# A planner's table of durations and its priorities set anew in a two-layer diffusion transformer kernel

## The chip, the core and the metric

The kernel runs on one core of a Trainium2 chip. The metric is the device time of one execution in microseconds (us), as the median of several runs. A core has five engines that each execute their own instructions strictly in order: TensorE (PE, matrix products into PSUM banks; its weight loads are listed as PEld), VectorE (DVE), ScalarE (ACT), GpSimd (POOL) and SyncE (SP), whose queue issues the transfers here. Engines wait for one another through semaphores, so an instruction that isn't ready holds up everything behind it on its engine.

## What is computed

Two layers over 512 latent and 256 context tokens of width 1024, with the same weights for both streams. The reference, cut to one layer's frame:

```python
m_lat = jnp.split(s_lat @ w_ada[li] + b_ada[li], 6, axis=-1)      # adaLN: six sections, also m_ctx
h = rms_norm(x, g_mix[li]) * (1.0 + m_lat[1]) + m_lat[0]
p = h @ w_in[li]                                                  # four groups of columns
y = jnp.concatenate([fourier_mix(..), diff_attention_latent(..), na_attention_latent(..), chunk_gmlp(..)], axis=-1)
x = x + m_lat[2] * (y @ w_out[li])
h = rms_norm(x, g_ffn[li]) * (1.0 + m_lat[4]) + m_lat[3]
x = x + m_lat[5] * conv_ffn(h, ffn_up[li], ffn_conv[li], ffn_conv_b[li], ffn_down[li])   # inner width 2816
```

The second layer needs the context only for its keys and values. Everything is float32; to keep that precision, a large product is three products of float32r operands, each operand being split into a high part and a low part.

## The kernel before

The streams lie feature-major in SBUF, eight tiles of 128 features. Products accumulate in eight PSUM banks. A product over 128 features is three matmuls (`mm3`: high by high, high by low, low by high).

**Weights.** `w_stream` fetches the weights in quarters of 128 x 512 into the four buffers `raw`. `w_split` makes the two parts of each in one of six pairs `wq`: ACT copies the high part, and a subtraction gives the low part, on DVE or POOL.

**adaLN.** `ada_wide` computes half a section of the modulation vectors on DVE, by product-sums over 128 x 512 tiles of the transposed weights. A tile serves one product-sum, or two where both streams need it. The tiles come through three buffers `wa`, one after another at a pace (`ada_loader`, first number of `pace` for layer 0 from a start time, last number for layer 1, begun with layer 0's FFN). In the trace such a product-sum is CUSTOM_DVE_ANT_0, with a short DVE_READ_ACCUMULATOR2_ANT behind it; in the listing of the order both are called ISA.

**Main stream.** One thread, `main`, walks through units in the order of the strings `o0` and `o1` (one for each layer): DQ, DK, DV are query, key and value projections of differential attention, NQ, NK, NV those of neighbourhood attention, GU and GV the two halves of the gating MLP, FA and FC the two halves of Fourier mixing, OO the out-projection. The letter behind says for which streams. The FFN follows, in 22 steps: `up` (two blocks of 128 channels), `conv` and `gated` on ACT, DVE and POOL, and now and then a `down` for four steps; `lead` says how many steps `up` runs ahead. The second layer's FFN begins in two halves of tokens, so its norm (`Norm`) has two parts: a sum of squares, a matmul with `ones`, a power on POOL (`mhalf`), a matmul that spreads the result over the partitions (`ident`), and then eight chunks that DVE and ACT scale, shift and split.

**Order.** Next to the main stream run threads for the results of each unit (`qk_post`, `copy_post`), attention items, gates, norms and weight splits. A thread offers one instruction at a time. The class `Sched` takes the thread whose instruction could start first by the planner's clock, or, among those that could start within `slack` of that, the one of the smallest number in `pr`. An instruction's duration in this plan is `Eng.cost`. Where the same work can go to two engines (`Alt`), the planned end plus a bias decides (`bias_w` for the weight subtractions: so many us are added to DVE's end). The instructions of each engine are then issued in the order of the plan; at run time only semaphores decide when they run. `items` and `heads` bound the attention items under way, `res_b` and `keep` hold back SBUF for them. All instructions are recorded in line 311 of the kernel before (line 314 of the changed one), so the trace is read by tiles, not by lines.

Of the kernel before, what the change touches and what calls it, by code (L numbers as in the profile page):

```python
# [11 lines left out]
F32R = mybir.dt.float32r  # L12
# [15 lines left out]
P = {"sb": 14016, "sr": 25920, "res_b": 1920, "res_r": 0, "res_p": 0, "heads": 2, "items": 8, "slack": 0.12,  # L28
     "pace": (5.5, 45.0, 6.5), "bias": {'DVE': 0.3}, "bias_w": {'DVE': 4.6}, "nk": 1,
     "st": (0, 0.2, 0, 0.3, 0.6, 0.4, 0.5),  # L30
     "pr": {'d': 1.5, 'n': 0.5, 'g': 2.11, 'gate': 3.5, 'w': 6.5, 'y': 0.01, 'conv': 0.51, 'gated': 0.01, 'main': 4.9, 'f': 3.5, 'fm': 7.7, 'ad': 0.01, 'an': 1.11, 'ada': 9.7},
     "o0": 'DKj4 DVj2 DQi GUj NKl FAj NKc GVj FCc NVl NQj NVc XX FCl OOc OOl',
     "o1": 'DKj2 GUl2 DQl DVj NKi NVi FAl NQl GVl XX FCl OOa OOb', "lead": 4, "ffn_s": (1, 0), "tail": [],
     "parts": [1, 1, 2], "uph": 2, "ada0": [[[1, 0, 1], [0, 0, 0]], [[1, 1, 1], [0, 1, 0]]], "seg": 0, "early": 1,
     "keep": 2080, "across": 1, "step": 4}
# [6 lines left out]
class Op:  # L42
    """One or more instructions of one engine, not yet issued."""
# [15 lines left out]
class Alt:  # L59
    """The same work on either of several engines."""  # L60
# [5 lines left out]
class Req:  # L66
    """A buffer of n elements per partition of an arena, wanted once some tiles have been written."""
# [6 lines left out]
class Arena:  # L74
    """Buffers of any length cut from one tile, short ones from its end."""
# [12 lines left out]
    def place(self, n, now):  # L88
        """The place for n grains that is free first, and when."""
# [83 lines left out]
class Eng:  # L173
    """An engine; its instructions come back as Ops."""
# [25 lines left out]
    def cost(self, op, aps, nkw, kw):  # L200
        n = max(elems(x) for x in aps)
        ps = any(x.tensor.name == self.psum for x in aps)
        if self.name == "PE":
            n = elems(aps[0])
            if op == "transpose":
                return 0.056 if aps[1].dtype == F32R else 0.11
            return max(0.109, n / 2400.0 + 0.0025) if aps[1].dtype == F32R else max(0.214, n / 597.0)
        if self.name == "DVE":
            if op == "tensor_copy":
                return 0.068 + n / (960.0 if ps else 1920.0)  # L210
# [1602 lines left out]
```

## Time and profile before

| what | value |
|---|---|
| median of 3 runs | 1694.07 us (1693.99 to 1695.23) |
| span of the profiled execution | 1691.7 us, 26998 instructions |
| PE busy | 1614.1 us, 95% |
| DVE busy | 1081.3 us, 64% |
| ACT busy | 753.5 us, 45% |
| POOL busy | 746.9 us, 44% |
| granted PE clock, mean | 0.981 of full speed |

The median is 2.4 us above the profiled span; that is what lies around the first and the last instruction. The mean shares hide the stages: the mixers of layer 0 end near 336 us, its out-projection at 446, its FFN at 1022; the mixers and the out-projection of layer 1 end near 1321, and its FFN fills the rest. A granted clock of 1.00 is 2.4 GHz and of 0.50 is 1.2 GHz; a stretch in between has had both.

### The profile page before, as it was taken

The numbers are of one execution on the slowest core, as the hardware profiler recorded it, in microseconds if no ns is written. First come the engines' busy times: TensorE is split into PE (matmuls) and PEld (weight loads), VectorE is DVE, ScalarE is ACT, GpSimd is POOL, SyncE is SP. The second block draws the span as 40 slices with busy tenths as digits, with TensorE's granted clock in tenths as the row PEclk, the third lists the DMA queues.
The fourth block names the chain that finished last, engine by engine and source line by source line (L and its number), as shares of the span: only waits on it lengthen the run. The fifth ranks groups of instructions, "written<-read, shape, count | busy, mean of one in ns | idle before, by whom it ended". The sixth has DMA issues, their size and how long they took to land.

```text
span 1691.7 us, 26998 instructions
## 1 busy us (share of the span) xinstructions
PE 1614.1 (95%) x9932; PEld 1431.5 (85%) x9932; DVE 1081.3 (64%) x2132; ACT 753.5 (45%) x1481; POOL 746.9 (44%) x585
## 2 busy tenths in 40 slices
PE   6889999999999999999999998899998999999999
PEld 2779988898788888888888888899998888888887
DVE  6989997797886555445454569697576544434334
ACT  3437663674433313233232335476675543433431
POOL 4782345526433333323233346632438744444442
PEclk9899999999999999999999998999999899999999
DMA  7432223445433333333333342410324433333232
GB/s 251 146 100 69 59 87 95 129 141 197 127 125 100 101 100 105 101 104 103 97 103 100 101 136 82 124 44 26 116 100 142 140 108 96 96 98 100 94 99 87
DMA packets 101652, 183.03 MB, mean 108 GB/s; under 512 B 12176, under 2 KB 14864, under 8 KB 101520
## 3 DMA queue, kind: packets, MB, share of 16 engines
q1 hardware_dynamic: 101520, 181.31, 34.1%
q8 instruction: 78, 1.28, 0.3%
q14 instruction: 54, 0.44, 0.1%
HBM read 177.07 MB, written 4.19 MB: 107 GB/s over the span
## 4 chain that ended last, share of the span: by engine, by line
PE 77%; DVE 14%; POOL 3%; DMA 2%; issue 2%; ACT 2%; SPq 0%; POOLq 0%; ACTq 0%; DVEq 0%
PE banks L311 77%; DVE plain L311 10%; DVE rounded L311 2%; POOL plain L311 2%; DVE wa L311 1%; DMA wa<-in_w_adat_dram 1%; ACT plain L311 1%; POOL wq L311 1%; DMA plain<-in_ctxT_dram 1%; ACT wq L311 0%; DMA raw<-in_w_out_dram 0%; DMA plain<-in_w_adat_dram 0%; SPq L311 0%; DVE banks L311 0%; ACT rounded L311 0%
## 5 line engine op out<-in xcount | busy, mean ns | idle before, releaser
L311 PE MATMUL banks<-rounded,wq 128*128 128x512 f32 (+2 forms) x5856 | 1101.6, 349 | 13.9 <-DVE rounded L311 4.5
L311 PEld LDWEIGHTS banks<-rounded,wq 128*128 128x128 f32 x5856 | 945.5, 190 | 155.8 <-DVE rounded L311 6.9
L311 POOL TENSOR_TENSOR wq<-raw,wq 128x512 fp32r<-128x512 f32 x425 | 573.1, 1355 | 690.9 <-ACT wq L311 669.8
L311 ACT ACTIVATE wq<-raw 128x512 fp32r<-128x512 f32 x425 | 263.7, 626 | 333.6 <-PE banks L311 252.5
L311 PE MATMUL banks<-wq,rounded 128*128 128x256 f32 (+1 forms) x1980 | 276.7, 295 | 14.3 <-DVE plain L311 5.8
L311 DVE SCALAR_TENSOR_TENSOR plain<-banks,conv,plain 128x769 f32<-128x769 f32 (+1 forms) x176 | 155.6, 884 | 204.4 <-ACT plain L311 201.5
L311 PEld LDWEIGHTS banks<-wq,rounded 128*128 128x128 f32 x1980 | 254.4, 197 | 25.6 <-DVE rounded L311 7.1
L311 DVE SCALAR_TENSOR_TENSOR plain<-banks,m,plain 128x512 f32<-128x512 f32 (+1 forms) x176 | 112.5, 640 | 168.8 <-PE banks L311 168.3
L311 DVE CUSTOM_DVE_ANT_0 wa<-wa,plain 128x512 f32<-128x512 f32 x160 | 149.5, 936 | 49.7 <-DMA wa<-in_w_adat_dram 47.6
L311 ACT ACTIVATE plain<-banks,conv 128x770 f32<-128x770 f32 (+1 forms) x88 | 78.1, 888 | 168.1 <-PE banks L311 168.1
L311 POOL TENSOR_TENSOR plain<-plain,mhalf 128x4 f32<-128x4 f32 (+2 forms) x74 | 94.8, 1284 | 128.7 <-DVE plain L311 83.3
L311 DVE TENSOR_TENSOR plain<-plain 128x256 f32<-128x256 f32 (+4 forms) x169 | 124.6, 740 | 32.8 <-ACT plain L311 15.2
L311 ACT ACTIVATE plain<-banks 128x256 f32<-128x256 f32 (+2 forms) x225 | 96.3, 443 | 105.1 <-PE banks L311 86.6
L311 ACT ACTIVATE plain<-banks,plain 128x64 f32<-128x64 f32 (+4 forms) x189 | 112.7, 606 | 50.0 <-DVE plain L311 24.8
L311 ACT ACTIVATE plain<-plain 128x256 f32<-128x256 f32 (+3 forms) x152 | 78.5, 535 | 96.6 <-DVE plain L311 87.5
L311 ACT ACTIVATE rounded<-plain 128x512 fp32r<-128x512 f32 (+2 forms) x112 | 69.8, 629 | 115.8 <-DVE plain L311 92.6
L311 DVE TENSOR_TENSOR rounded<-plain,rounded 128x256 fp32r<-128x256 f32 (+2 forms) x103 | 86.6, 847 | 28.6 <-ACT rounded L311 27.7
L311 DVE CUSTOM_DVE_ANT_0 plain<-wa,plain 128x512 f32<-128x512 f32 x96 | 82.4, 858 | 29.8 <-DMA wa<-in_w_adat_dram 29.6
L311 DVE TENSOR_REDUCE plain<-banks 128x1 f32<-128x768 f32 (+4 forms) x112 | 91.9, 834 | 11.2 <-PE banks L311 8.4
L311 PE MATMUL banks<-plain 128*128 128x64 f32 x736 | 91.6, 273 | 2.7 <-DVE plain L311 2.2
L311 PEld LDWEIGHTS banks<-plain 128*128 128x128 f32 x736 | 89.3, 193 | 5.0 <-DVE plain L311 2.5
L311 PE MATMUL banks<-ident,plain 128*128 128x128 f32 (+1 forms) x496 | 80.2, 280 | 12.3 <-DVE plain L311 7.0
(68 smaller groups left out, 892.0 us busy)
## 6 DMA issues: line engine op xcount, KB each, us to landing
raw<-in_ffn_up_dram SPq DMA_DIRECT2D x184, 256.0 KB, 2.6
wa<-in_w_adat_dram SPq DMA_DIRECT2D x160, 256.0 KB, 2.9
raw<-in_ffn_down_dram SPq DMA_DIRECT2D x88, 256.0 KB, 2.6
raw<-in_w_in_dram SPq DMA_DIRECT2D x80, 256.0 KB, 2.8
raw<-in_w_out_dram SPq DMA_DIRECT2D x64, 256.0 KB, 2.8
plain<-in_na_bias_dram SPq DMA_DIRECT2D x16, 320.0 KB, 3.9
plain<-in_xT_dram SPq DMA_DIRECT2D x16, 256.0 KB, 4.5
plain<-in_w_ada_dram SPq DMA_DIRECT2D x16, 256.0 KB, 3.7
```

The costliest lines, as they stand in the source:

```text
L311: fn(*args, **kw)
```

## The change

No instruction is added or taken away. Numbers of the table `P` and formulas of `Eng.cost` change, and with them the order and the choice between DVE and POOL (or ACT and DVE). Removed comments are left out of the diff.

```diff
-P = {"sb": 14016, "sr": 25920, "res_b": 1920, "res_r": 0, "res_p": 0, "heads": 2, "items": 8, "slack": 0.12,
-     "pace": (5.5, 45.0, 6.5), "bias": {'DVE': 0.3}, "bias_w": {'DVE': 4.6}, "nk": 1,
...
-     "o0": 'DKj4 DVj2 DQi GUj NKl FAj NKc GVj FCc NVl NQj NVc XX FCl OOc OOl',
-     "o1": 'DKj2 GUl2 DQl DVj NKi NVi FAl NQl GVl XX FCl OOa OOb', "lead": 4, "ffn_s": (1, 0), "tail": [],
...
-     "keep": 2080, "across": 1, "step": 4}
+P = {'sb': 14016, 'sr': 25920, 'res_b': 640, 'res_r': 0, 'res_p': 0, 'heads': 2, 'items': 4, 'slack': 0.1,
+     'pace': (5.5, 64.2, 4.1), 'bias': {'DVE': 0.3}, 'bias_w': {'DVE': 1.0}, 'nk': 1,
...
+     'o0': 'DKj4 DVj2 DQi GUj NKl NKc NVc NVl FAj FCc GVj NQj XX FCl OOc OOl',
+     'o1': 'DKj2 DQl DVj NVi GVl NQl NKi GUl2 FAl XX FCl OOa OOb', 'lead': 5, 'ffn_s': [1, 0], 'tail': [],
...
+     'keep': 1024, 'across': 1, 'step': 4}
...
             if op == "transpose":
-                return 0.056 if aps[1].dtype == F32R else 0.11
-            return max(0.109, n / 2400.0 + 0.0025) if aps[1].dtype == F32R else max(0.214, n / 597.0)
+                return 0.064 if aps[1].dtype == F32R else 0.11
+            return max(0.06, n / 2350.0 + 0.0095) if aps[1].dtype == F32R else max(0.112, n / 590.0)
         if self.name == "DVE":
+            two = 1.0 if ps else 1.25
...
             if op == "tensor_tensor_reduce":
-                return 0.09 + n / 960.0
+                return 0.18 + n * two / 960.0
...
         if self.name == "ACT":
-            return (0.05 if ps else 0.094) + n / 1200.0 + 0.093 * (nkw + ("accum_out" in kw))
+            return (0.1 if ps else 0.15) + n / 1200.0 + 0.093 * (nkw + ("accum_out" in kw))
         if self.name == "DMA":
-            return max(0.475, n * 128 * 4 / 360e3)
+            return max(0.475, n * 128 * 4 / 340e3)
         if ALU.pow in kw.values() or n <= 16:
-            return 0.3 + 0.165 * n
-        return 0.15 + n / 476.0
+            return 0.45 + 0.165 * n
+        return 0.2 + n / 450.0
```

The other DVE formulas (copies, scalar and two-input operations) get the factor `two` or a slope of 1600 for 1920 elements; all fourteen priorities in `pr` have new values, of which the product-sums' (`ada`) goes from 9.7 to 8.75, the main stream's from 4.9 to 8.4 and attention's from 0.01 and 1.11 to 0.48 and 0.01.

What this does to the order is shown in three places. First VectorE in the FFN of layer 0, a stretch of an early step up to the split of its gated product (`rounded<-plain,rounded 128x770`). Before:

```order
L311 SCALAR_TENSOR_TENSOR plain<-banks,conv,plain 128x769 x2
L311 ISA plain<-wa,plain 128x512
L311 ISA plain 128x1
L311 TENSOR_TENSOR plain<-plain 128x770
L311 ISA wa,plain<-wa,plain 128x512
L311 ISA plain 128x1
L311 TENSOR_TENSOR rounded<-plain,rounded 128x770
```

On the same engine, the same kind of stretch in the changed order:

```order
L314 SCALAR_TENSOR_TENSOR plain<-banks,conv,plain 128x769
L314 ISA plain<-wa,plain 128x512
L314 ISA plain 128x1
L314 ISA wa,plain<-wa,plain 128x512
L314 ISA plain 128x1
L314 ISA plain<-wa,plain 128x512
L314 ISA plain 128x1
L314 ISA wa,plain<-wa,plain 128x512
L314 ISA plain 128x1
L314 TENSOR_TENSOR rounded<-plain,rounded 128x770
```

Four product-sums stand where two stood, and the multiplication of the gate by the value went to POOL in this step. Second TensorE at the opening of layer 1: `ones` and `ident` are the norm's two products, `wq,rounded 128x256` the projections, `identr` the transposes of K and Q ahead of the first attention head, `rounded 128x512` its scores. Before:

```order
L311 MATMUL banks<-ones,plain 128x1 x6
L311 MATMUL banks<-ident,plain 128x128 x6
L311 MATMUL banks<-wq,rounded 128x256 x414
L311 MATMUL banks<-identr,rounded 96x128 x20
L311 MATMUL banks<-wq,rounded 128x256 x72
L311 MATMUL banks<-identr,rounded 96x128 x20
L311 MATMUL banks<-wq,rounded 128x256 x6
L311 MATMUL banks<-rounded 128x512
```

And in the changed order:

```order
L314 MATMUL banks<-ones,plain 128x1 x6
L314 MATMUL banks<-ident,plain 128x128 x6
L314 MATMUL banks<-wq,rounded 128x256 x294
L314 MATMUL banks<-identr,rounded 96x128 x20
L314 MATMUL banks<-wq,rounded 128x256 x90
L314 MATMUL banks<-rounded,wq 128x512 x6
L314 MATMUL banks<-identr,rounded 96x128 x20
L314 MATMUL banks<-rounded,wq 128x512 x6
L314 MATMUL banks<-rounded 128x512
```

The first transposes come 120 projection matmuls sooner, since the gate units now stand behind the attention's. Third TensorE at the end of layer 1's mixers and the start of its FFN: `rounded,wq 128x256` are the out-projection and the first steps of `up` for half the tokens, `ones` and `ident` the norm of the first and then of the second half. Before:

```order
L311 MATMUL banks<-rounded,wq 128x256 x195
L311 MATMUL banks<-ones,plain 128x1 x2
L311 MATMUL banks<-rounded,wq 128x256 x18
L311 MATMUL banks<-ident,plain 128x128 x2
L311 MATMUL banks<-rounded,wq 128x256 x174
L311 MATMUL banks<-ones,plain 128x1 x2
L311 MATMUL banks<-rounded,wq 128x256 x48
L311 MATMUL banks<-ident,plain 128x128 x2
L311 MATMUL banks<-rounded,wq 128x256 x129
```

And in the changed order:

```order
L314 MATMUL banks<-rounded,wq 128x256 x210
L314 MATMUL banks<-ones,plain 128x1 x2
L314 MATMUL banks<-rounded,wq 128x256 x24
L314 MATMUL banks<-ident,plain 128x128 x2
L314 MATMUL banks<-rounded,wq 128x256 x165
L314 MATMUL banks<-ones,plain 128x1 x2
L314 MATMUL banks<-rounded,wq 128x256 x18
L314 MATMUL banks<-ident,plain 128x128 x2
L314 MATMUL banks<-rounded,wq 128x256 x159
```

For the second half the spreading product stands 18 matmuls behind the sum instead of 48; for the first half 24 instead of 18.

Over the whole kernel 35 of the 425 weight subtractions go from POOL to DVE (none was DVE's before); PE and SP have as many instructions as before.

## Rows read from the trace of the kernel before

**Rows 1.** Busy time by stage: start:end, length, then us of each engine; PEclk, DMA, GB/s.
```profile
43.50:121.40 77.90, 63.99 (x465) 58.26 (x464) 74.62 (x167) 31.48 (x64) 59.97 (x43) 0.92 0.39 120
121.40:336.50 215.10, 202.12 (x1532) 189.99 (x1533) 188.24 (x493) 133.74 (x343) 93.61 (x80) 0.96 0.29 89
336.50:446.00 109.50, 106.57 (x726) 96.91 (x725) 92.31 (x193) 61.14 (x139) 49.73 (x37) 1.00 0.52 167
446.00:474.00 28.00, 22.35 (x113) 18.04 (x112) 25.92 (x46) 12.79 (x20) 9.98 (x7) 0.88 0.37 109
474.00:995.00 521.00, 521.00 (x2980) 459.89 (x2979) 277.24 (x457) 153.60 (x213) 164.49 (x124) 1.00 0.33 103
995.00:1092.00 97.00, 85.39 (x621) 80.74 (x620) 77.56 (x167) 48.22 (x96) 62.55 (x47) 0.95 0.34 108
1321.00:1350.00 29.00, 25.42 (x178) 24.15 (x179) 15.80 (x25) 16.88 (x30) 21.76 (x18) 0.88 0.46 136
```

The five engines of these rows are PE, PEld, DVE, ACT and POOL.

**Rows 2.** PE's waits in the whole span: us in total, times, longest.
```profile
PE banks L311 <- DVE plain L311: 34.0, 22, 5.0
```

**Rows 3.** Timeline at 446: start, us, engine, operation, idle time before and its releaser.
```profile
446.66 1.29 POOL L311 TENSOR_TENSOR wq<-raw,wq 128x512 fp32r<-128x512 f32 x1 [1.10 <-ACT wq L311]
446.80 1.70 DVE L311 CUSTOM_DVE_ANT_0 plain<-wa,plain 128x512 f32<-128x512 f32 x1
...
448.54 0.69 DVE L311 CUSTOM_DVE_ANT_0 wa<-wa,plain 128x512 f32<-128x512 f32 x1
```

**Rows 4.** Groups by shape, whole span: count, busy us, mean ns of one, idle before.
```profile
L311 DVE CUSTOM_DVE_ANT_0 wa<-wa,plain 128x512 f32<-128x512 f32 x160 | 149.5, 936 | 49.7 <-DMA wa<-in_w_adat_dram 47.6
...
L311 DVE TENSOR_TENSOR plain<-plain 128x256 f32<-128x256 f32 x85 | 57.3, 675 | 28.1 <-POOL plain L311 13.9 <-ACT plain L311 13.6
L311 DVE TENSOR_TENSOR rounded<-plain,rounded 128x512 fp32r<-128x512 f32 x35 | 38.9, 1111 | 13.1 <-ACT rounded L311 12.8
...
L311 POOL TENSOR_TENSOR wq<-raw,wq 128x512 fp32r<-128x512 f32 x425 | 573.1, 1355 | 690.9 <-ACT wq L311 669.8 <-PE banks L311 15.3 <-issue 4.2
```

**Rows 5.** Timeline of PE at the first transposes of layer 0.
```profile
120.23 0.56 PE L311 MATMUL banks<-identr,rounded 128*96 128x128 f32 x3 [5.02 <-DVE plain L311]
```

**Rows 6.** Busy time by stage, three steps of layer 0's FFN, columns as in rows 1.
```profile
474.00:490.70 16.70, 16.70 (x98) 14.81 (x97) 15.69 (x35) 7.20 (x10) 4.71 (x4) 1.00 0.49 151
490.70:507.40 16.70, 16.70 (x98) 14.81 (x97) 12.14 (x19) 5.99 (x8) 6.63 (x5) 1.00 0.29 94
...
557.50:574.00 16.50, 16.50 (x97) 14.65 (x96) 8.87 (x15) 5.99 (x8) 5.29 (x4) 1.00 0.36 111
```

**Rows 7.** The same view, only DVE's instructions on `wa` tiles, three stretches.
```profile
490.70:507.40 16.70, 5.70 (x5) 1.00 0.29 94
...
557.50:574.00 16.50, 3.18 (x5) 1.00 0.36 111
995.00:1092.00 97.00, 13.47 (x12) 0.95 0.34 108
```

**Rows 8.** Timeline of DVE at the opening of layer 1.
```profile
1061.75 1.80 DVE L311 CUSTOM_DVE_ANT_0 wa<-wa,plain 128x512 f32<-128x512 f32 x1 [2.12 <-DMA wa<-in_w_adat_dram]
...
1082.91 0.43 DVE L311 TENSOR_TENSOR rounded<-plain,rounded 128x256 fp32r<-128x256 f32 x1 [0.70 <-ACT rounded L311]
```

**Rows 9.** Timeline of PE at the opening of layer 1.
```profile
1065.83 7.54 PE L311 MATMUL banks<-wq,rounded 128*128 128x256 f32 x61 [3.52 <-DVE plain L311]
```

**Rows 10.** Timeline of DVE at the start of layer 1's FFN.
```profile
1321.14 0.16 DVE L311 TENSOR_SCALAR plain<-banks 128x2 f32<-128x2 f32 x1 [0.70 <-PE banks L311]
1327.92 3.30 DVE L311 SCALAR_TENSOR_TENSOR plain<-plain,ga 128x256 f32<-128x256 f32 x4 [6.62 <-ACT plain L311]
```

**Rows 11.** Timeline of POOL at the start of layer 1's FFN.
```profile
1320.50 5.03 POOL L311 TENSOR_TENSOR wq<-raw,wq 128x512 fp32r<-128x512 f32 x4 [0.34 <-ACT wq L311]
1325.49 0.71 POOL L311 TENSOR_TENSOR plain<-plain,mhalf 128x2 f32<-128x2 f32 x1
```

**Rows 12.** Timeline of PE in the mixers of layer 1, attention's f32 products.
```profile
1243.20 3.01 PE L311 MATMUL banks<-plain 128*128 128x64 f32 x26
```

More of the change, by code (lines that the diff above doesn't have):

```diff
@@ L27 @@
 NEG = -1.0e30
[L28 to L35 removed]
+P = {'sb': 14016, 'sr': 25920, 'res_b': 640, 'res_r': 0, 'res_p': 0, 'heads': 2, 'items': 4, 'slack': 0.1,
+     'pace': (5.5, 64.2, 4.1), 'bias': {'DVE': 0.3}, 'bias_w': {'DVE': 1.0}, 'nk': 1,
+     'st': [0, 0.2, 0, 0.3, 0.6, 0.4, 0.5],
+     'pr': {'d': 5.88, 'n': 0.01, 'g': 7.6, 'gate': 6.26, 'w': 5.94, 'y': 6.97, 'conv': 2.77, 'gated': 8.24, 'main': 8.4, 'f': 2.81, 'fm': 3.04, 'ad': 0.48, 'an': 0.01, 'ada': 8.75},
+     'o0': 'DKj4 DVj2 DQi GUj NKl NKc NVc NVl FAj FCc GVj NQj XX FCl OOc OOl',
+     'o1': 'DKj2 DQl DVj NVi GVl NQl NKi GUl2 FAl XX FCl OOa OOb', 'lead': 5, 'ffn_s': [1, 0], 'tail': [],
+     'parts': [1, 1, 2], 'uph': 2, 'ada0': [[[1, 0, 1], [0, 0, 0]], [[1, 1, 1], [0, 1, 0]]], 'seg': 0, 'early': 1,
+     'keep': 1024, 'across': 1, 'step': 4}
 NBLK = 4
@@ L205, in cost @@
             if op == "transpose":
-                return 0.056 if aps[1].dtype == F32R else 0.11
-            return max(0.109, n / 2400.0 + 0.0025) if aps[1].dtype == F32R else max(0.214, n / 597.0)
+                return 0.064 if aps[1].dtype == F32R else 0.11
+            return max(0.06, n / 2350.0 + 0.0095) if aps[1].dtype == F32R else max(0.112, n / 590.0)
         if self.name == "DVE":
+            two = 1.0 if ps else 1.25
             if op == "tensor_copy":
-                return 0.068 + n / (960.0 if ps else 1920.0)
+                return 0.068 + n / (960.0 if ps else 1600.0)
             if op == "tensor_scalar":
-                return 0.07 + n / 960.0 if n < 32 else 0.13 + n / (960.0 if ps else 1920.0)
+                return 0.07 + n / 960.0 if n < 32 else 0.13 + n / (960.0 if ps else 1600.0)
             if op == "tensor_tensor_reduce":
-                return 0.09 + n / 960.0
+                return 0.18 + n * two / 960.0
             if op == "scalar_tensor_tensor":
-                return 0.13 + n / 960.0
-            return 0.068 + n / 960.0
+                return 0.13 + n * two / 960.0
+            if op == "tensor_reduce":
+                return 0.1 + n / 960.0
+            return 0.068 + n * two / 960.0
         if self.name == "ACT":
-            return (0.05 if ps else 0.094) + n / 1200.0 + 0.093 * (nkw + ("accum_out" in kw))
+            return (0.1 if ps else 0.15) + n / 1200.0 + 0.093 * (nkw + ("accum_out" in kw))
         if self.name == "DMA":
-            return max(0.475, n * 128 * 4 / 360e3)
+            return max(0.475, n * 128 * 4 / 340e3)
         if ALU.pow in kw.values() or n <= 16:
-            return 0.3 + 0.165 * n
-        return 0.15 + n / 476.0
+            return 0.45 + 0.165 * n
+        return 0.2 + n / 450.0
 class Thread:
```

## The prediction

> **What bounds the kernel now.** The page's busy shares put TensorE (PE) far ahead of the others, but a busy PE is no PE at full speed, and the share hides where it idles. So I went to the stages. The table by stage [rows 1] says where the waste lies. In each row, the length less PE's busy time is idle time, and the length times one minus PEclk is what the half clock cost. Mixers of layer 0 (43.5 to 336.5): 26.9 us idle, 14.8 us of clock. Out-projection of layer 0: 2.9. Start of its FFN (446 to 474): 5.6 and 3.4. The FFN of layer 0 (474 to 995): nothing; PE is the bound and stays it. Opening of layer 1 (995 to 1092): 11.6 and 4.9. Start of its FFN (1321 to 1350): 3.6 and 3.5. So an order can win something in 43 to 474 and in 995 to 1350, and can only lose in the FFN.
>
> What does PE wait for? VectorE (DVE): 34.0 us in the largest row [rows 2]. DVE is busy 74.62 of 77.9 us and then 188.24 of 215.1 us in layer 0's mixers [rows 1]: there DVE is as much the bound as PE. Part of its busy time is a wait of another kind: a 512-element product-sum took 0.69 us with GpSimd (POOL) idle and 1.70 us when it started 0.14 us after a POOL subtraction [rows 3]. That is why the product-sum's mean is 936 ns and the 512-element subtraction's on DVE 1111 ns [rows 4].
>
> **The change part by part.** Each engine still executes in order what the planner recorded, so a changed number works only by moving an instruction or giving it to another engine. Counted in the two orders:
>
> *Mixers of layer 0.* Up to DVE's first residual of the out-projection, DVE has 855 instructions before and 812 now: 20 product-sums of adaLN (100 to 80) and their 20 accumulator reads go behind, 10 weight subtractions come over from POOL, and 13 others leave. With [rows 4]: 20 x 0.94 = 18.8 us less, 10 x 1.11 = 11.1 us more, 13 x 0.68 = 8.8 us less (most are 256-element sums): DVE is 16.5 us shorter. POOL has 10 x 1.36 = 13.6 us less there; at 59.97 of 77.9 us it was nearly full in the first part [rows 1]. DVE was busy for 90% of the 293 us, so most of the 16.5 us should show; a part stays in chains through other engines. I take -12. The upper bound is all of it with part of the clock's loss, -20. The other bound: the transposes for the first attention, which waited 5.02 us for DVE [rows 5], have 12 projection matmuls more ahead (12 x 0.12 = 1.5 us) but two subtractions more on DVE (2.2 us), and if the later units of the order wait likewise the stage ends +2.
>
> *Opening, before 43.5.* DVE's 32 product-sums from the full stream stay; 16 multiplies by the norm factor go mostly to POOL. 0, from -2 to +3.
>
> *Out-projection of layer 0.* Its idle time is 2.9 us and DVE comes to it with less behind: -1 (-3 to 0).
>
> *Start of layer 0's FFN.* The last shift of adaLN that the chunks need is now finished between the norm's sum and its first chunk instead of before, about 1 us of DVE work more in the path (a product-sum and two small adds), while fewer product-sums stand among the chunks: +1 (-2 to +4).
>
> *FFN of layer 0.* What was moved out of the mixers lands here: 108 product-sums between DVE's first and last convolution there before, 153 now, and nearly all in the first six steps, 13 a step where 5 stood. A step is 16.7 us of matmuls; in it DVE was busy 8.87 us [rows 6], of which 3.18 were product-sums [rows 7]. With 8 more, 8.87 + 8 x 0.94 = 16.4 us: full, but not over. The step from 474 had 15.69 us on DVE, and PE lost nothing [rows 6]. At the 12.14 us of the heaviest later step (5.70 of it product-sums, five of them), 19.7 us, 3 over. The cover is what PE has in its free PSUM banks and in split weights; if it goes, the loss is the excess. +1 (0 to +10).
>
> *Opening of layer 1.* The other end of the new pace: 22 product-sums stood in DVE's queue between the FFN and the first attention of this layer, none now. In 995 to 1092 twelve took 13.47 us [rows 7], and one of them made DVE wait 2.12 us for its tile and then took 1.80, after which PE had waited 3.52 us [rows 8, 9]. These stalls go: about -5 with the clock that they cost. Against it, PE's queue ahead of the first transposes of K and Q loses the gate units (96 matmuls) and 24 more, 414 before and 294 now. Q's last matmul was the 48th of the run that begins at 1065.83 with 7.54/61 = 0.124 us each, so it ended near 1071.8, and Q's last part was written at 1082.91 + 0.43 = 1083.3, 11.5 us later [rows 8, 9]. The other 78 matmuls of the 414 filled that time; now 54 do (6.5 us): a wait of 5, less some 2 for the two product-sums in that tail. And six weight subtractions are DVE's in this stretch, 6 x 1.11 = 6.7 us in a queue that was busy for 80%, for units that PE takes next; half of it shows. -5 + 3 + 3.5 = +1.5, taken as +2; from -6 (all cover holds) to +9 (none does).
>
> *Rest of layer 1's mixers.* Attention ends sooner, which takes fillers from the last Fourier step, but its queue on POOL loses some 20 subtractions to DVE. 0 (-4 to +4).
>
> *Start of layer 1's FFN.* The norm's sum reached DVE at 1321.14; the power that follows stood on POOL behind four subtractions, ended at 1326.2, and DVE's first chunk ran at 1327.92, after 6.62 us idle [rows 10, 11]. In the new order one of these subtractions is DVE's and the power is the next on POOL; on PE the product that spreads the result stands 30 matmuls (3.6 us) earlier. That stage wastes 7.1 us: -4 (-6 to 0).
>
> Sum: -12 + 0 - 1 + 1 + 1 + 2 + 0 - 4 = -13 us. From the profiled span of 1691.7 this gives 1678.7; the runs' median of 1694.07 has 2.4 us around the span, which stay: **1681 us**.
>
> **The rivals.**
> *More comes back.* The 35 subtractions that leave POOL occupied it for 35 x 1.355 = 47 us, and whatever DVE had in that time was held up, by 1.0 us in the pair shown [rows 3]. If DVE loses those waits as well, each moved subtraction costs it 0.69 us (its neighbour's time with POOL idle) instead of 1.11 and spares it one wait: 35 x 0.42 = 15 us, and about as much again if half of the 35 had met a DVE operation. With half of that 32 us in stages where DVE bounds, another -16: 1665. The Trainium skill, SBUF — State Buffer, section on the two separate sides, says that the port pair of DVE and GpSimd is an exclusive lock for a whole instruction, and the loser waits; the pair of 0.69 and 1.70 us agrees. For it: the pair. Against it: with POOL still busy for some 700 us, a DVE subtraction meets the next POOL one.
>
> *Nothing comes of it.* The new durations are not all nearer the trace. An f32 matmul of 64 columns leaves two records, and 26 took 3.01 us [rows 12], so one takes 0.23 us; the planner had 0.214 and now has 0.112. It thinks attention's products half as long on PE and can set them where others wait behind. The order has 368 such; if one in ten made DVE's turn late by its own 0.23 us and the head of the queue waited a further instruction, some 10 us return: 1691.
>
> *Slower.* The place is the FFN of layer 0, steps 1 to 6. If the product-sums there take the 1.11 us of the contended kind rather than 0.94, and the steps' other work is as in the heaviest one (12.14 - 5.70 = 6.4 us, [rows 6, 7]), then 13 x 1.11 + 6.4 = 20.8 us, 4.1 over the step, 25 us in six; PE pays that as soon as the lag exceeds the banks it can fill ahead. With -14 from the other terms: 1694 - 14 + 25 = 1705; with half the cover holding, 1692. It decides from a DVE load of 16.7 us a step. For it: the count, and that a tile's transfer in the same queue as the weights waits for DVE. Against it: the step from 474.
>
> **How the numbers follow.** The forecast (1672 to 1690) 0.50; more comes back (under 1672) 0.17; nothing (1690 to 1698) 0.13, of which 0.09 lie within 0.2% (3.4 us, about what a measurement of this kernel can tell from no change); slower by the FFN 0.12; slower otherwise (layer 1's opening at its full +9 and more, with the mixers' gain lost) 0.08. Faster: 0.50 + 0.17 + 0.03 = 0.70; same 0.09; slower 0.12 + 0.08 + 0.01 = 0.21. The range leaves out a tenth on each side: below, what lies under the 1665 of the first rival; above, the full loss in the FFN: 1664 to 1702.
>
> **What would show it.** Right: DVE's busy time in the mixers of layer 0 falls by some 15 us and PE's end of the out-projection comes 10 to 15 us sooner; the product-sums vanish from layer 1's opening; the 6.62 us idle time ahead of the chunks at layer 1's FFN shrinks below 4. Wrong: PE's idle time in 474 to 600 is above 3 us (the FFN term), the first transposes of layer 1 wait over 9 us, or DVE is still full up to 336 because its operations got longer. What breaks the forecast most easily is the first term: if the 16.5 us less on DVE don't reach PE, the sum is about -1.

## The result and the profile after

The changed kernel takes 1666.3 us (median; 1666.2 to 1668.1), the one before 1694.0 beside it: ratio 0.9837, with a 95% interval of 0.9823 to 0.9851. That is 27.7 us less. The forecast was 13 us less: the right direction and about half the size. The profiled execution spans 1664.6 us for 1691.7, so 27.1 us are to be found in the traces.

Busy time by stage after the change, with the columns of [rows 1] (start:end, length, then PE, PEld, DVE, ACT, POOL, PEclk, DMA share, GB/s). The stages are cut at the same instructions as those of before, the first matmul of a unit, and so begin at other times:

```profile
43.50:110.60 67.10, 59.52 (x443) 55.89 (x444) 63.02 (x148) 30.97 (x60) 49.94 (x37) 0.90 0.34 111
110.60:311.60 201.00, 195.93 (x1572) 186.14 (x1571) 178.58 (x464) 137.84 (x353) 95.34 (x81) 1.00 0.27 87
311.60:416.20 104.60, 103.39 (x709) 94.95 (x708) 87.46 (x191) 58.21 (x131) 45.66 (x33) 1.00 0.51 171
416.20:446.30 30.10, 22.38 (x114) 18.54 (x113) 26.18 (x53) 15.38 (x25) 7.63 (x6) 0.89 0.33 101
446.30:977.30 531.00, 522.68 (x2978) 457.31 (x2977) 320.84 (x542) 147.10 (x208) 184.94 (x130) 1.00 0.36 115
977.30:1062.80 85.50, 75.95 (x525) 72.00 (x524) 65.03 (x147) 44.59 (x89) 48.76 (x35) 0.90 0.22 74
```

The same stretch of the mixers before, from the first matmul of the gate units to the first of the out-projection:

```profile
113.00:336.50 223.50, 204.62 (x1553) 192.01 (x1554) 196.57 (x508) 137.76 (x352) 101.83 (x86) 0.95 0.29 88
```

Three things are to be seen. In the mixers of layer 0 (second row) PE is now busy for 195.9 of 201.0 us at full clock; before it was busy for 204.6 of 223.5 at 0.95. In the FFN of layer 0 (fifth row), where PE idled for nothing before, 531.0 us pass and PE is busy for 522.7. And the opening of layer 1 (last row) needs 85.5 us; before, 97.0 ([rows 1], 995 to 1092) with the 11.5 us of the gate units in it, which the new order puts later: the same.

PE's waits over the whole span, as in [rows 2]:

```profile
PE banks L314 <- DVE plain L314: 23.5, 17, 3.5
PE banks L314 <- DMA plain<-in_w_ada_dram: 10.3, 8, 4.0
PE banks L314 <- DVE rounded L314: 10.1, 10, 3.3
...
PE banks L314 <- DVE wq L314: 3.0, 2, 2.3
```

The waits for DVE's `plain` results went from 34.0 to 23.5 us; 8.1 of the 23.5 are new ones in the FFN. The last row is a wait that didn't exist before: for a weight subtraction on DVE.

Where the 27.1 us come from, each stage's length in the two profiled executions (us) beside the term of the prediction:

| stage | before | after | difference | predicted |
|---|---|---|---|---|
| up to the first gate unit of layer 0 | 113.0 | 110.6 | -2.4 | 0 and part of -12 |
| rest of layer 0's mixers | 223.5 | 201.0 | -22.5 | -12 |
| out-projection | 109.4 | 104.6 | -4.8 | -1 |
| start of the FFN (first step) | 28.2 | 30.1 | +1.9 | +1 |
| FFN of layer 0, further steps | 520.7 | 531.0 | +10.3 | +1 |
| opening of layer 1, gate units left out | 85.7 | 85.5 | -0.2 | +2 |
| rest of layer 1 up to its FFN | 238.2 | 233.9 | -4.3 | 0 |
| FFN of layer 1 to the end | 373.0 | 367.9 | -5.1 | -4 |

### The profile page after: what moved, and what is told of

It reads as the page before. It is cut to its first block, busy times and chain, and to the rows that moved or that the text cites. A ratio compares the mean times of both kernels' runs of the same rounds, so it can differ in the third digit from the quotient of the medians.

```text
span 1664.6 us, 27016 instructions
## 1 busy us (share of the span) xinstructions
PE 1599.3 (96%) x9932; PEld 1419.3 (85%) x9932; DVE 1103.6 (66%) x2170; ACT 749.1 (45%) x1478; POOL 715.3 (43%) x550
## 4 chain that ended last, share of the span: by engine, by line
PE 75%; DVE 16%; DMA 3%; ACT 2%; issue 2%; POOL 1%; SPq 0%; ACTq 0%; POOLq 0%; DVEq 0%
PE banks L314 75%; DVE plain L314 10%; DVE wa L314 3%; DVE rounded L314 2%; ACT plain L314 1%; POOL wq L314 1%; DMA raw<-in_w_out_dram 1%; DMA wa<-in_w_adat_dram 1%; DVE wq L314 1%; SPq L314 0%; DMA plain<-in_w_adat_dram 0%; ACT wq L314 0%; DMA raw<-in_ffn_up_dram 0%; ACT rounded L314 0%; POOL plain L314 0%
## 5 line engine op out<-in xcount | busy, mean ns | idle before, releaser
L314 POOL TENSOR_TENSOR wq<-raw,wq 128x512 fp32r<-128x512 f32 x390 | 528.2, 1358 | 709.5 <-ACT wq L314 675.3
L314 DVE CUSTOM_DVE_ANT_0 wa<-wa,plain 128x512 f32<-128x512 f32 x160 | 140.3, 878 | 45.3 <-DMA wa<-in_w_adat_dram 43.6
L314 POOL TENSOR_TENSOR plain<-plain,mhalf 128x4 f32<-128x4 f32 (+2 forms) x74 | 95.7, 1298 | 119.2 <-DVE plain L314 92.0
L314 ACT ACTIVATE plain<-banks,plain 128x768 f32<-128x768 f32 (+4 forms) x189 | 112.9, 606 | 54.9 <-PE banks L314 39.7
L314 DVE TENSOR_TENSOR plain<-plain 128x256 f32<-128x256 f32 (+4 forms) x166 | 110.8, 670 | 19.7 <-ACT plain L314 13.0
L314 ACT ACTIVATE rounded<-plain 128x512 fp32r<-128x512 f32 (+2 forms) x110 | 65.7, 603 | 82.5 <-DVE plain L314 58.1
L314 DVE TENSOR_TENSOR rounded<-plain,rounded 128x256 fp32r<-128x256 f32 (+2 forms) x108 | 88.2, 823 | 17.3 <-ACT rounded L314 16.4
L314 DVE CUSTOM_DVE_ANT_0 plain<-wa,plain 128x512 f32<-128x512 f32 x96 | 86.5, 902 | 15.8 <-DMA wa<-in_w_adat_dram 15.7
L314 POOL TENSOR_TENSOR plain<-plain 128x256 f32<-128x256 f32 (+2 forms) x52 | 61.7, 1196 | 61.8 <-DVE plain L314 27.8
```

Of the source, the lines that this page charges most:

```text
L314: fn(*args, **kw)
```

## The experiments

Each experiment is a short edit of one of the two kernels. Since a planner sets the order, an edit of its numbers changes the whole order; an edit that leaves the plan alone and changes only what an instruction does keeps it. Both kinds were needed. A ratio below is the run's time over that of the kernel before, measured beside it, with the 95% interval in brackets. Lengths of stages in the experiments' traces (us), cut at the same instructions; the columns from the opening to the FFN are layer 0's:

| run | opening | mixers | out-projection | FFN start | FFN | layer 1 to its FFN | rest |
|---|---|---|---|---|---|---|---|
| before | 113.0 | 223.5 | 109.4 | 28.2 | 520.7 | 323.9 | 373.0 |
| changed | 110.6 | 201.0 | 104.6 | 30.1 | 531.0 | 319.4 | 367.9 |
| e1 | 112.0 | 225.4 | 106.1 | 29.9 | 518.7 | 322.9 | 372.8 |
| e2 | 115.0 | 220.7 | 119.2 | 28.2 | 527.1 | 319.5 | 372.5 |
| e3 | 121.1 | 221.2 | 110.7 | 35.2 | 520.9 | 338.5 | 374.5 |
| e4 | 111.3 | 213.7 | 113.8 | 28.8 | 525.7 | 327.2 | 370.2 |
| e5 | 102.8 | 211.2 | 107.5 | 27.1 | 520.8 | 324.9 | 372.9 |
| e6 | 110.8 | 201.1 | 104.5 | 30.7 | 520.5 | 318.7 | 367.8 |
| e7 | 111.0 | 206.8 | 108.6 | 27.8 | 520.5 | 322.3 | 373.4 |
| e8 | 111.6 | 200.9 | 104.6 | 31.0 | 524.4 | 316.5 | 367.9 |
| e9 | 111.0 | 204.5 | 108.0 | 30.6 | 532.3 | 319.7 | 371.0 |
| e10 | 116.8 | 201.9 | 107.6 | 44.5 | 527.4 | 321.1 | 374.1 |
| e11 | 112.9 | 200.5 | 104.7 | 32.0 | 531.0 | 328.2 | 370.4 |
| e12 | 111.9 | 201.2 | 104.6 | 30.9 | 529.0 | 347.1 | 369.1 |
| e13 | 110.8 | 201.0 | 104.6 | 30.9 | 525.5 | 321.4 | 367.8 |
| e15 | 107.2 | 198.8 | 104.5 | 29.0 | 523.5 | 317.6 | 367.8 |

### One part of the change alone (e1 to e4)

Theory A was mine: VectorE's load sets the end of layer 0's mixers, and the change shortens it. Rivals: the order of the projections (B), the truer durations (C).

e1, the new order of layer 0's projections in the kernel before:

```diff
-     "o0": 'DKj4 DVj2 DQi GUj NKl FAj NKc GVj FCc NVl NQj NVc XX FCl OOc OOl',
+     "o0": 'DKj4 DVj2 DQi GUj NKl NKc NVc NVl FAj FCc GVj NQj XX FCl OOc OOl',
```

> The kernel before with the new order of layer 0's projections alone (old durations, priorities, pace, biases). Theory A, VectorE's load sets the end of layer 0's mixers: product-sums of adaLN ahead of the out-projection stay at 112, so its start stays within 4 us of 336.5 and the time within 5 us of the kernel before. Rival B, the order of the projections (attention's K and V ahead of the Fourier unit) keeps TensorE fed: start of the out-projection 15 to 25 us sooner, time 1670 to 1680.

Measured: ratio 0.9979 (0.9969 to 0.9990), mixers 225.4 us. The out-projection began at 337.4 us, within the 4 us of theory A; the new order by itself did nothing for the mixers, and B as a cause by itself falls.

e2, the new pace of the adaLN tiles alone:

```diff
-     "pace": (5.5, 45.0, 6.5), "bias": {'DVE': 0.3}, "bias_w": {'DVE': 4.6}, "nk": 1,
+     "pace": (5.5, 64.2, 4.1), "bias": {'DVE': 0.3}, "bias_w": {'DVE': 4.6}, "nk": 1,
```

> The kernel before with the new pace of the adaLN tiles alone (start 64.2 for 45, 4.1 for 6.5 us in layer 1's sections). Ahead of the out-projection of layer 0 stand 98 product-sums for 112. Theory A: its start comes 14 x 0.94 = 13 us sooner and somewhat more with the clock (-13 to -18), the FFN of layer 0 gives back 5 to 10 us, layer 1's opening gains some 5: time 1676 to 1688. Rival B: start of the out-projection within 4 us of before, time 1692 to 1702 by the loss in the FFN. Rival C (the new durations): the same as B.

Measured: ratio 1.0053 (1.0038 to 1.0068), slower. The out-projection began 0.8 us sooner, not 13 to 18, so theory A missed here. Of the 14 product-sums that go, 6 leave the opening, which gets 2.0 us longer; 8 leave the mixers, which get 2.8 us shorter, and the out-projection takes 119.2 us, since more of the attention is left for it. The 6.4 us lost in the FFN are as expected. So moving product-sums out of the way is not enough.

e3, the new durations of `Eng.cost` in the kernel before; e4, the old ones in the changed kernel. The edit is the diff of `cost` above, one way and the other.

> The kernel before with the new durations of the planner alone. Rival C, that an order planned with truer durations waits less: start of the out-projection of layer 0 at least 10 us sooner, time under 1684. Theory A: 109 product-sums for 112 and no weight subtraction moved, so at most 3 us sooner there, and the time within 6 us of before.

> The changed kernel with the planner's old durations, so the new table, orders and priorities without the new durations. Ahead of the out-projection of layer 0 stand 100 product-sums (89 in the changed kernel, 112 before) and 14 weight subtractions on VectorE (9 and 0). Theory A: 12 x 0.94 - 14 x 1.11 = 4 us more than before at worst, so about half or less of the changed kernel's gain in the mixers, time 1675 to 1690. Rival C: the gain is lost, time over 1690. Rival B: the gain in the mixers stays whole, time under 1672.

Measured: e3 has ratio 1.0158 (1.0139 to 1.0177) and is 26 us slower than before, which neither theory had. e4 has 0.9956 (0.9939 to 0.9972), a quarter of the gain, with mixers of 213.7 us; theory A's range holds. So C as a rule that truer durations always help falls: in these two plans the new durations go with a gain beside the new table and with a loss beside the old one. Each of them is a single plan, and the nudges below show how far single plans scatter.

### Less work in an unchanged order (e5, e6, e15)

In these three the plan is the same as in the kernel they come from, instruction by instruction; the product-sums of one layer's adaLN read half a tile. That leaves half of each sum out, so these kernels compute wrong vectors; they serve for the time alone. The edit for layer 0 (e5, e15); e6 has `li == 1`:

```diff
+                if li == 0:
+                    h = V.tensor_tensor_reduce((t if st == ns - 1 else prod)[:, 0:256], t[:, 0:256],
+                                               sbc[0][:, st * D + (i % 2) * 512:st * D + (i % 2) * 512 + 256], 1.0, 0.0,
+                                               ALU.mult, ALU.add, accum_out=acc[:, i % 2, i // 2, st:st + 1])
+                    h.cost = o.cost
```

> The kernel before in exactly its order, but layer 0's product-sums of adaLN run over 256 of each tile's 512 columns (so its modulation vectors are left incomplete); the planner still counts them whole. Of VectorE's work ahead of the out-projection 112 product-sums get shorter by 0.27 to 0.3 us, some 30 us. Theory A, VectorE's load sets the end of the mixers one to one: the out-projection starts 20 to 30 us sooner than 336.5, the time falls by 20 to 32. Rival B, TensorE waits because the order doesn't fit (an instruction at the head of its queue whose inputs come late by chains through other engines): under 10 us.

> The changed kernel in exactly its order, but layer 1's product-sums, nearly all of which stand in the first steps of layer 0's FFN, run over 256 of 512 columns (layer 1's modulation vectors are left incomplete). In the changed kernel 531 us pass from the second step's first matmul to the last group of the FFN, 521 before. If those 10 us are VectorE's load of 13 product-sums a step: 520 to 523, time 8 to 11 us less than the changed kernel's. If it is the tiles' transfers in the queue of the weights or the new lead: within 3 us.

> The changed kernel in its order, with layer 0's product-sums over 256 of 512 columns (its modulation vectors are left incomplete), as e5 for the kernel before. If VectorE's load still bounds the mixers at the rate of e5 (0.6 us for each us less on it, from the gate units to the out-projection): some 16 us less on it and that stretch 8 to 10 us shorter, time 1650 to 1657. If the changed order has made TensorE the bound there: under 4 us in that stretch, time over 1658.

Measured: e5 has ratio 0.9849 (0.9834 to 0.9864), e6 0.9780 (0.9762 to 0.9797) with 1656.1 us, e15 0.9733 (0.9716 to 0.9750) with 1649.9 us. The rows of the stages, first the mixers of e5 and then those of e15, with the columns as above:

```profile
102.80:314.00 211.20, 199.53 (x1556) 188.61 (x1555) 175.11 (x507) 137.13 (x351) 97.11 (x86) 0.97 0.30 93
```

```profile
107.20:306.00 198.80, 195.34 (x1572) 186.03 (x1570) 167.18 (x462) 137.37 (x353) 91.62 (x81) 1.00 0.29 88
```

In the old order DVE's busy time fell from 196.57 to 175.11 us and the stretch from 223.5 to 211.2: 12.3 us for 21.5, or 0.57 for one. So VectorE's load did bound it, though not one to one. (From the start of the kernel to the out-projection it was 22.5 us for 33.6, or 0.67 for one, within the 20 to 30 us of theory A.) In the changed order the same edit took 178.58 to 167.18 and the stretch from 201.0 to 198.8: 2.2 for 11.4, or 0.19 for one. In the changed order VectorE, busy for 89% of the stretch, hardly bounds it any more; PE does, with 195.9 us of work in 201.0. That is what e15's second alternative had for the stretch (under 4 us). Its time fell below both alternatives all the same, since 3.4 us came back in the opening and 7.5 in the FFN, where the last product-sums of layer 0 stand.

Load and order can also be told apart by pairs of plans in which VectorE does nearly the same work in the mixers. First e3 (old table) and e7 (new table and durations but for one price), then e10 (a plan of the changed kernel, below), which stands beside the row of e5:

```profile
121.10:342.30 221.20, 203.76 (x1528) 192.04 (x1527) 186.53 (x483) 131.94 (x329) 100.04 (x84) 0.93 0.26 81
111.00:317.80 206.80, 200.09 (x1586) 189.49 (x1585) 185.65 (x492) 140.52 (x364) 88.12 (x75) 0.99 0.30 95
116.80:318.70 201.90, 196.17 (x1565) 186.17 (x1563) 175.18 (x457) 137.46 (x351) 91.82 (x78) 1.00 0.28 84
```

With VectorE busy for 186.5 and 185.7 us the stretch takes 221.2 and 206.8 us and PE idles for 17.4 and 6.7; with 175.1 (e5) and 175.2 it takes 211.2 and 201.9 and PE idles for 11.7 and 5.7. At equal load the new table's plans are 14 and 9 us shorter.

e6 settles the FFN. Its row for the same stretch as the fifth row above:

```profile
447.10:967.60 520.50, 520.50 (x2978) 457.91 (x2977) 280.71 (x542) 148.86 (x208) 176.77 (x130) 1.00 0.37 117
```

The order is that of the changed kernel, DVE has 40 us less to do, and PE's idle time is gone, as the first alternative had it. The 10 us are the product-sums' load on VectorE, not the tiles' transfers nor `lead`, which are unchanged in e6.

### Two numbers changed on purpose (e7, e8, e13, e14)

e7 mends the planner's price of an f32 matmul, e8 slows the tiles of layer 1, e13 also begins them later; e14 is the changed kernel beside e13 and e15.

```diff
-            return max(0.06, n / 2350.0 + 0.0095) if aps[1].dtype == F32R else max(0.112, n / 590.0)
+            return max(0.06, n / 2350.0 + 0.0095) if aps[1].dtype == F32R else max(0.214, n / 590.0)
...
-     'pace': (5.5, 64.2, 4.1), 'bias': {'DVE': 0.3}, 'bias_w': {'DVE': 1.0}, 'nk': 1,
+     'pace': (5.5, 64.2, 5.5), 'bias': {'DVE': 0.3}, 'bias_w': {'DVE': 1.0}, 'nk': 1,
...
-                         PR["ada"], P["pace"][2]), PR["ada"])
+                         PR["ada"], P["pace"][2], sch.now + 35.0), PR["ada"])
```

> The changed kernel with one duration of the planner nearer the trace: an f32 matmul of 64 columns counts 0.214 us for 0.112. Its order has 101 product-sums and 10 weight subtractions on VectorE ahead of layer 0's out-projection (89 and 9 in the changed kernel). Theory A: 12 x 0.94 + 1.1 = 12 us more there, time 1672 to 1682. Rival C, that truer durations make the better order: 1664 or less.

> The changed kernel with layer 1's adaLN tiles at 5.5 us for 4.1, so some 9 product-sums a step of layer 0's FFN for 13, and still all of them ahead of layer 1. If the 10 us lost in that FFN are VectorE's load: the loss falls to 3 or less, time 1656 to 1661. If a changed number acts by shuffling the rest of the plan: anywhere from 1660 to 1675, with layer 1's stages moved.

> The changed kernel with layer 1's adaLN tiles at 5.5 us for 4.1 (as e8) and begun 35 us later in the plan, so that they don't compete with the last tiles of layer 0 at the start of its FFN. The 10 us lost in the FFN of layer 0 should shrink to 2 or less (e8: 3.7) and the FFN's start (30 us in the changed kernel, 31 in e8) to 28: time 1654 to 1659, under the changed kernel and under e8. If the FFN's start is late for another reason: 1658 to 1663.

> The changed kernel itself, beside the other two on the same chip: 1664 to 1669.

Measured: e7 takes 1672.5 us, ratio 0.9878 (0.9864 to 0.9893), as theory A had it and not C. The truer price makes a kernel that is 6 us slower. It loses in the mixers of layer 0 (206.8 us for 201.0, with 12 product-sums more), in the out-projection there (108.6 for 104.6) and in the second layer's FFN (373.4 for 367.9); the FFN of layer 0 with 14 fewer gives 10.5 us back.

e8 takes 1661.2 us, 0.9812 (0.9792 to 0.9832). Its FFN of layer 0 takes 524.4 us for 531.0, so 3.7 us are still lost against the kernel before, where 3 or less were expected. e13 takes 1664.2 us, 0.9820 (0.9804 to 0.9836), beside e14 with 1667.1 us, 0.9839 (0.9825 to 0.9853), and missed both of its alternatives: its FFN takes 525.5 us, and the start of it still 30.9, so the tiles of layer 1 are not what makes that start long. Both versions are the fastest whole kernels of the study, by 3 to 5 us; their intervals overlap that of the changed kernel, so it isn't settled that they are faster.

### Nudges that mean nothing to the chip (e9, e10)

```diff
-P = {'sb': 14016, 'sr': 25920, 'res_b': 640, 'res_r': 0, 'res_p': 0, 'heads': 2, 'items': 4, 'slack': 0.1,
+P = {'sb': 14016, 'sr': 25920, 'res_b': 640, 'res_r': 0, 'res_p': 0, 'heads': 2, 'items': 4, 'slack': 0.101,
...
-            return (0.1 if ps else 0.15) + n / 1200.0 + 0.093 * (nkw + ("accum_out" in kw))
+            return (0.102 if ps else 0.152) + n / 1200.0 + 0.093 * (nkw + ("accum_out" in kw))
```

> The changed kernel with the planner's slack at 0.101 for 0.100 us: a number with no meaning for the chip, whose plan differs in a few places of layer 0 and more in layer 1 (89 product-sums and 9 weight subtractions on VectorE ahead of layer 0's out-projection, as in the changed kernel). If the order's fit in the mixers of layer 0 comes from the durations and the table: out-projection at 311 to 314, time 1663 to 1670. If it is the luck of one plan: out-projection later than 316, time over 1672.

> The changed kernel with ScalarE's planned time 2 ns longer for each instruction, which the trace can't tell from the changed kernel's; the plan differs nearly everywhere, with VectorE's load ahead of the out-projection of layer 0 the same (89 product-sums, 8 subtractions). As before: fit by the durations and the table, out-projection at 310 to 316, time 1661 to 1672; luck of one plan, later than 318, time over 1675.

Measured: e9 takes 1675.3 us, 0.9881 (0.9861 to 0.9902), e10 1695.3 us, 1.0005 (0.9996 to 1.0014). Both times are those of the alternative "luck of one plan". The start of the out-projection, the other sign, came at 315.5 us in e9, between the two alternatives, and at 318.7 in e10, where luck begins; but in e10 the delay stands in the opening (116.8 us for 110.6). Two nanoseconds on the planned time of ScalarE's instructions cost the whole gain. Yet the mixers take 204.5 and 201.9 us in these plans, and 206.8 in e7: that part of the gain, 17 to 22 us of the 223.5, is there in every plan made here with the new table and the new durations (in e7 but for one price). Most of what is lost is lost elsewhere, in e10 half of it at the start of layer 0's FFN, 44.5 us for 30.1. Timeline of PE there, then of DVE (start, us, engine, operation, idle time before and its releaser):

```profile
435.11 2.08 PE L314 MATMUL banks<-ident,plain 128*128 128x128 f32 x8 [1.86 <-POOL plain L314]
450.57 2.01 PE L314 MATMUL banks<-rounded,wq 128*128 128x258 f32 x6 [13.38 <-DVE rounded L314]
```

```profile
448.87 0.69 DVE L314 CUSTOM_DVE_ANT_0 plain<-wa,plain 128x512 f32<-128x512 f32 x1
...
449.48 0.17 DVE L314 TENSOR_TENSOR m<-plain,b_ada 128x8 f32<-128x8 f32 x1
...
450.55 0.43 DVE L314 TENSOR_TENSOR rounded<-plain,rounded 128x256 fp32r<-128x256 f32 x1
```

PE waits 13.38 us for a chunk of the norm, which needs the second half of the shifts, a half section of layer 0's adaLN; its last addition (`m`) runs at 449.48, behind a product-sum of the section after. In the changed kernel the same addition runs 1.1 us ahead of the spreading product, just in time; in e10's plan it runs 14 us behind it:

```profile
423.80 0.16 DVE L314 TENSOR_TENSOR m<-plain,b_ada 128x8 f32<-128x8 f32 x1
```

```profile
424.93 2.08 PE L314 MATMUL banks<-ident,plain 128*128 128x128 f32 x8 [2.03 <-POOL plain L314]
```

The later start of the tiles (64.2 for 45 us) is not enough to explain it. In e2, which has it too, the addition ran at 434.35 us, 20.5 us ahead of that FFN, and in e7 27 us ahead; in e10 9 us of the norm's other chunks stand in VectorE's queue ahead of the section's last product-sums. It is the plan again.

The two nudges bear on all runs whose plan differs from that of the kernel they come from (e1 to e4, e7, e12): a difference of up to some 30 us between two such plans can be the fit of one plan and need not be the effect of the number that was changed.

### Two parts undone in the changed kernel (e11, e12)

e11 lets the 35 subtractions run on POOL again, at the places in the plan where VectorE had them; e12 takes back layer 1's order.

```diff
-        yield sub(lo, t, hi, bias=P["bias_w"])
+        alt = sub(lo, t, hi, bias=P["bias_w"])
+        alt.ops[0].calls = alt.ops[1].calls
+        yield alt
...
-     'o1': 'DKj2 DQl DVj NVi GVl NQl NKi GUl2 FAl XX FCl OOa OOb', 'lead': 5, 'ffn_s': [1, 0], 'tail': [],
+     'o1': 'DKj2 GUl2 DQl DVj NKi NVi FAl NQl GVl XX FCl OOa OOb', 'lead': 5, 'ffn_s': [1, 0], 'tail': [],
```

> The changed kernel in its order, but its 35 weight subtractions of VectorE run on POOL, at the same places of the plan, as all did before. Theory A: ahead of layer 0's out-projection VectorE loses 9 x 0.9 = 8 us; at two thirds of a microsecond for one (e5) that stage ends 5 us sooner, unless what POOL gains (9 x 1.36 = 12 us) holds it up. In layer 1, POOL is full again: the out-projection and the first steps of the FFN lose 3 to 6 us. Sum -2 to +3. If the port the two share is what the change relieved: slower in both layers, time over 1675.

> The changed kernel with layer 1's projections in the order of the kernel before; layer 0 is the same plan. My steps gave that order no gain (+2 in the opening, 0 in the rest): time 1662 to 1668. If the order of layer 1 carries a part of the gain: 1670 or more.

Measured: e11 takes 1678.1 us, 0.9902 (0.9887 to 0.9917), so the moved subtractions are worth 12 us of the 28 in this order, where I had expected -2 to +3. They are worth nothing in the mixers of layer 0 (200.5 for 201.0), where I had counted them as a cost of 11.1 us on VectorE, and 11.3 us in layer 1 (328.2 for 319.4 and 370.4 for 367.9). PE's waits there, from the first matmul of K to the FFN, in e11 and then in the changed kernel:

```profile
PE banks L314 <- DVE plain L314: 6.1, 3, 4.1
PE banks L314 <- POOL wq L314: 5.6, 2, 4.6
```

```profile
PE banks L314 <- DVE plain L314: 3.5, 3, 1.4
PE banks L314 <- DVE wq L314: 3.0, 2, 2.3
```

In e11 PE waits 5.6 us for weights from POOL; in the changed kernel 3.0 us for the same weights from VectorE; these two rows account for 5.2 of the 8.8 us lost ahead of layer 1's FFN.

e12 takes 1696.8 us, 1.0013 (1.0003 to 1.0022), where I had expected 1662 to 1668: all the gain is gone, in layer 1 alone (347.1 us for 319.4). The rows of that stretch, e12 and then the changed kernel:

```profile
977.60:1324.70 347.10, 324.35 (x2353) 305.02 (x2352) 233.49 (x496) 196.96 (x430) 139.38 (x115) 0.92 0.24 77
977.30:1296.70 319.40, 305.26 (x2353) 292.75 (x2352) 234.18 (x503) 195.69 (x430) 139.05 (x109) 0.97 0.25 84
```

Of the 27.7 us, 8.6 are idle time of PE, and 19.1 are the same matmuls at a lower mean clock, 0.92 for 0.97. In the old table the same order of layer 1 took 323.9 us, so in this plan an order that did well with the old priorities does badly with the new ones.

Not tried: the old order of layer 0 within the changed table. So which of the table's entries (priorities, `items`, reserves, order) carries the mixers' gain stays open.

## Why the prediction was right in direction and half in size

**The mixers of layer 0: the term that failed.** I put -12 there, with -20 as the bound, and found -22.5, with 2.4 more in the opening. The count of VectorE's work was good: 16.5 us less expected; DVE was busy for 293.2 us up to the out-projection before and for 272.6 now, 20.6 less (23 product-sums fewer, where I had counted 20, and nine subtractions for ten). The discount was good as well: e5 gives 0.57 us for each us of VectorE's load in the old order, so the 18.0 us less in that stretch account for some 10.

What I had no term for is the order itself. I argued that a changed number works "only by moving an instruction or giving it to another engine", and then priced only the work that left VectorE, not the fit of what stayed: which PE instruction stands at the head when VectorE's result arrives. The remaining 12 us I put down to that. The size comes by subtraction; that there is such an effect, and of about this size, is shown by the pairs of plans with equal load on VectorE, 9 and 14 us apart, and e15 shows that in the changed order the load hardly matters. Which entry of the table makes the better fit stays open.

The clock has its part in this. Of the 22.5 us, 13.8 are PE's idle time (18.9 to 5.1 us) and 8.7 are busy time that got shorter (204.62 to 195.93 us), while the granted clock rose from 0.95 to 1.00; I had counted the clock in the bound of -20 only. In the trace of before a sign was there: 223.5 us with PE idle for 18.9 and DVE idle for 26.9 us. Where two engines both idle in a stretch, neither's load is the whole bound, and a better order can win from both.

**The out-projection**, -4.8 for -1. It had 722 matmul records of its stage before, 706 now; more of the attention runs ahead of it. e1, with nothing new but the order of the projections, has the same shift (704 records) and an out-projection of 106.1 us, so this too is the order of what stays and not load taken off VectorE.

**The FFN of layer 0**, +10.3 for +1: the other mis-sized term, at the upper end of the range given (0 to +10) where I had valued it near the lower. The mechanism was the one I named as a rival, and PE's idle time there, 8.3 us, is over the 3 that I had set as a sign of being wrong. A step of the changed kernel, then its product-sums alone:

```profile
519.30:538.30 19.00, 17.24 (x96) 14.60 (x97) 18.97 (x37) 5.61 (x9) 8.93 (x5) 1.00 0.47 149
```

```profile
519.30:538.30 19.00, 10.29 (x14) 1.00 0.47 149
```

VectorE is busy for 18.97 us in a step of some 17 us of matmuls, and PE waits once in each of five steps, 8.1 us in all; three of them:

```profile
500.50 17.07 PE L314 MATMUL banks<-rounded,wq 128*128 128x258 f32 x96 [1.70 <-DVE plain L314]
519.28 17.31 PE L314 MATMUL banks<-rounded,wq 128*128 128x258 f32 x96 [1.71 <-DVE plain L314]
538.33 17.33 PE L314 MATMUL banks<-rounded,wq 128*128 128x258 f32 x96 [1.74 <-DVE plain L314]
```

I had computed 16.4 to 19.7 us a step and trusted the lower, because the step from 474 had 15.69 us and cost nothing [rows 6]. One such step cost nothing; five in a row cost 1.5 to 1.7 us each. That free banks cover a single step is a guess that no run isolates.

**The opening of layer 1**, -0.2 for +2. The product-sums are gone, as counted. The first transposes did not wait at all, where I had 3 us; instead PE waited for weights that VectorE split, the third part of that sum:

```profile
1040.47 0.97 PE L314 MATMUL banks<-wq,rounded 128*128 128x256 f32 x6 [0.72 <-DVE wq L314]
1043.70 7.08 PE L314 MATMUL banks<-wq,rounded 128*128 128x256 f32 x35 [2.25 <-DVE wq L314]
1050.62 1.52 PE L314 MATMUL banks<-identr,rounded 128*96 128x128 f32 x20
```

**The rest of layer 1 and the start of its FFN**, -4.3 and -5.1 for 0 and -4. DVE and POOL at that start, as in [rows 10, 11]:

```profile
1299.72 0.16 DVE L314 TENSOR_SCALAR plain<-banks 128x2 f32<-128x2 f32 x1 [0.77 <-PE banks L314]
1301.14 0.94 DVE L314 TENSOR_TENSOR wq<-raw,wq 128x512 fp32r<-128x512 f32 x1 [1.26 <-ACT wq L314]
1303.85 3.12 DVE L314 SCALAR_TENSOR_TENSOR plain<-plain,ga 128x256 f32<-128x256 f32 x5 [1.77 <-ACT plain L314]
```

```profile
1300.23 1.30 POOL L314 TENSOR_TENSOR wq<-raw,wq 128x512 fp32r<-128x512 f32 x1 [0.15 <-ACT wq L314]
1301.48 1.15 POOL L314 TENSOR_TENSOR plain<-plain,mhalf 128x2 f32<-128x2 f32 x1
```

The power stands behind one subtraction instead of four, and the first chunk runs 4.1 us after the norm's sum instead of 6.8. This step came out as forecast, but its cause is the power's place in the order and hardly the subtraction that went to VectorE. In e11 all subtractions are on POOL again, and the chunk still runs 4.4 us after the sum:

```profile
1313.79 0.16 DVE L314 TENSOR_SCALAR plain<-banks 128x2 f32<-128x2 f32 x1 [0.89 <-PE banks L314]
1318.23 3.11 DVE L314 SCALAR_TENSOR_TENSOR plain<-plain,ga 128x256 f32<-128x256 f32 x5 [4.28 <-ACT plain L314]
```

Of the 11.3 us that layer 1 loses in e11, 8.8 stand before its FFN, in the stretch that I had put at 0.

**The rivals.** "More comes back" had the size (1665) but not the cause: its mechanism was the waits between POOL and VectorE, and taking the subtractions off VectorE again (e11) changed nothing in the mixers of layer 0; what it changed in layer 1 shows as PE's waits for weights. "Nothing comes of it" rested on the halved price of f32 matmuls: e7 mends it and is slower, so, as far as one plan can tell, that price did no harm here. "Slower" named the right place with a price of up to 25 us; 10 came.

**The chances.** I treated the change as a sum of mechanisms. The changed kernel, e9 and e10 have plans whose numbers differ by less than a trace can tell, and they take 1666, 1675 and 1695 us. The 1666.3 of the changed table is the best of the three, so a part of the 27.7 us is luck of the draw, and with it the right direction: e10 would have shown no gain. What all of them keep is 17 to 22 us in the mixers, which come with the table and durations together; the rest is the fit of one plan. That neighbours scatter by 10 to 30 us could have been known only from such runs, not from a trace.

## What to carry to other kernels

Before pricing a move off a busy engine, look whether the engine that waits and the engine it waits for both idle in that stretch: then load alone is not the bound, and a reordering can give more than the load taken away. Work pushed into a stage that TensorE fills is free only until the sum per step passes the step's length; take the per-step sum over several steps in a row, not one step that got away. And where a planner's numbers set the order, run one or two meaningless nudges of them before giving a cause for a gain: what survives the nudges (here the mixers) belongs to the change, the rest to the draw.

## What was not expected of the hardware

The waits between POOL and VectorE go on as before, on the moved subtractions too. In the changed kernel one on VectorE took 0.68 us and the next, which ran while POOL did the same work from 1312.83 to 1314.17, 1.42 us; it ended 0.56 us after POOL's:

```profile
1311.61 0.68 DVE L314 TENSOR_TENSOR wq<-raw,wq 128x512 fp32r<-128x512 f32 x1
...
1313.31 1.42 DVE L314 TENSOR_TENSOR wq<-raw,wq 128x512 fp32r<-128x512 f32 x1 [0.29 <-ACT wq L314]
```

The Trainium skill, SBUF — State Buffer, section on the two separate sides, describes a lock that one of the two holds for a whole instruction; the trace agrees with that, as 0.56 us after POOL's end is most of the 0.68 us that the subtraction takes alone. Unexpected is how little it mattered: without and with six such subtractions on VectorE the mixers of layer 0 took 200.5 (e11) and 201.0 us.
